# The forgetting heads' bias: a running sum on VectorE instead of a bias matmul per score block

## The chip, the core and the metric

The kernel runs on one core of one Trainium2 chip. A core has several engines that work side by side, each through its own list of instructions in order: TensorE (PE, matrix products, with its weight loads shown apart as PEld), VectorE (DVE), ScalarE (ACT), GpSimd (POOL), and SyncE (SP), which here does nothing but start transfers between DRAM and the on-chip memory SBUF. Matrix products end in PSUM, eight banks of 128 partitions by 512 numbers. The metric is the device time of one execution in microseconds; less is better.

## The reference

One layer of a hybrid sequence mixer, on 512 frames of width 2048, in float32. The normalised input is projected into three branches of four heads each (head width 128). Branch A is forgetting attention, the one that this change is in:

```python
log_f = jax.nn.log_sigmoid(f_logit)            # one logit per frame and head
c = jnp.cumsum(log_f, axis=1)                  # over the frames
logits = q @ k.T * scale                       # per block of 128 queries, keys 0..hi
logits = logits + c[lo:hi, None] - c[None, :hi]
logits = jnp.where(mask, logits, NEG)          # causal
o = softmax(logits) @ v
```

So the score of query t and key s carries c[t] − c[s], where c is the running sum of the log forget gates. Branch B is chunked attention with a learned bias by relative distance; branch C is stick-breaking attention. Each branch output is multiplied by the SiLU of a gate path and projected up to 2048 channels (the up stage), the three are merged with sigmoid gates, and one output projection with a residual ends the layer.

## The kernel before, in words

Activations lie with channels on the 128 partitions and the 512 frames along the free axis, so a tile is 128 by 512. Float32 accuracy is reached by splitting a number into a rounded part and a rest: ScalarE writes the rounded part (`hi`, line 243), VectorE the rest (`lo`, line 247), and a product is hi·hi + hi·lo + lo·hi. Nearly all of the vector and scalar work is these splits, of the weights above all: `wh` and `wl` for each weight tile `raw` that SP (or POOL, for tiles that are added together on their way) brings from DRAM. The large products run in pairs of column blocks with a Strassen-like scheme; line 262 holds their matmuls.

The program's order on PE, ACT and DVE is written out by a planner, `Flow`. Each piece of work is a Python generator that yields what it needs next: an event, slots of a pool, or an engine and a cost estimate. At every step the planner takes the piece that can start first on its engine. Pools of slots limit what is alive: 21 tiles of 256 KB (`t2s`), four PSUM banks for attention (`atts`), and others for weights and for the parts of the activations. Weight tiles form one long list of units; heads, gates and other work are hung at points of that list.

The stages in time: the start (to about 65 us), four C heads, four B heads (about 420 to 760 us), four A heads (about 760 to 1045 us), the up stage (to about 1205 us), and the output projections. Within the heads the score work is a small part between large projections, which fill TensorE. In the up stage each of 16 channel blocks is multiplied by its gate (line 1417) and summed over the branches (line 1424); two blocks are merged into a pair (`merged_a`, `merged_b`: the tiles `m`, `mt`, `mu`), which the output projections read.

The bias of an A head was made like this. `forget_bias` (in the first C head) writes the log forget gates of all heads to DRAM, `fd2`. `forget_sums`, shortly before the first A head, reads them, sums along the frames with a scan on VectorE (line 854), splits the sums, and lays them out in two tiles that stay to the end of the program: `crl` and `crb`. Rows 0 to 63 and 64 to 127 of these hold the parts of c and rows of ones, so that a product of the two, limited to one head's rows, gives c[t] − c[s]. `soft_start`, once per A head, makes that limit: `cr` is `crb` scaled on ScalarE by the head's column of a one-hot table `ohf` (line 968). `soft_scores`, once per block of 128 queries with m = 128, 256, 384 or 512 keys, issues the three matmuls of the scores, the bias matmul of `crl` and `cr` (line 992), the mask matmul (line 993, bfloat16), the row maximum on VectorE straight from PSUM (line 996), and the exponential on ScalarE from PSUM into `p` (line 998). A later division scales `p` (line 1014), and TensorE transposes it (line 1025).

A B head has no bias matmul: it fetches a tile `tb` of biases (256 KB) on SP, and one fused operation on VectorE adds `tb` to the scores, writes the sum to `p` in SBUF and gives the row maximum (line 1003, two instructions in the trace); line 1005 negates the maximum, and the exponential reads `p` (line 1008).

Of the kernel before, what the change touches and what calls it, by code (L numbers as in the profile page):

```python
# [12 lines left out]
ALU = mybir.AluOpType  # L13
# [49 lines left out]
class Flow:  # L63
# [16 lines left out]
    def give(self, slots, n=1):  # L80
        slots.free += [self.fin] * n
# [80 lines left out]
def hybrid_kernel(  # L162
# [34 lines left out]
    def t2(s, dt=F32):  # L197
        return tp.tile([P, S], dt, tag="t2", name=nm(s))
# [38 lines left out]
    def pair_of(name, dt=F32R):  # L237
        return t2(name + "h", dt), t2(name + "l", dt)
# [92 lines left out]

    ohf = cp.tile([P, NH], F32, name="ohf")
    nc.gpsimd.memset(ohf, 0.0)
    for r in range(4):
        nc.gpsimd.affine_select(out=ohf[32 * r:32 * r + 32, :], in_=ohf[32 * r:32 * r + 32, :],
                                pattern=[[1, NH]], base=0, channel_multiplier=-1,
                                compare_op=ALU.not_equal, fill=1.0)
# [470 lines left out]
    bias, bias_ev, f_ev, f2_ev = {}, Event(), Event(), Event()  # L808
    fd, fd2 = dp.tile([2 * NH, S], F32, name="fd"), dp.tile([NH, S], F32, name="fd2")

    def forget_bias():
# [25 lines left out]
        yield DVE, 3 * q  # L837
        nc.vector.scalar_tensor_tensor(p, p, 1.0, s, op0=ALU.add, op1=ALU.mult)
        nc.vector.tensor_scalar_mul(p, p, 2.0)
        nc.vector.scalar_tensor_tensor(v, v, 0.0, p, op0=ALU.min, op1=ALU.subtract)  # L840
        nc.sync.dma_start(fd2.rearrange("h (c t) -> (h c) t", t=T), v)
        f2_ev.t = flow.fin + 3.0

    def forget_sums():
        yield f2_ev
        yield t2s, 3
        v, s, u = t2("fv"), t2("fs"), t2("fu")
        nc.gpsimd.memset(v, 0.0)
        nc.gpsimd.memset(u, 1.0)
        for r in range(4):  # L850
# [3 lines left out]
        nc.vector.tensor_tensor_scan(s, u, v, 0.0, op0=ALU.mult, op1=ALU.add)  # L854
        give(t2s)
        yield t2s, 2
        hi, lo = pair_of("c")
        yield from split(hi, lo, s, S)
        give(t2s)
        yield t2s, 2  # L860
        crl, crb = t2("crl", F32R), t2("crb")
        a = ACT, act_us(S)
        yield a
        nc.scalar.activation(crl[0:32, :], f(hi[0:32, :]), AF.Copy)
        yield a
        nc.scalar.activation(crl[32:64, :], f(lo[32:64, :]), AF.Copy)
        yield a
        nc.scalar.activation(crl[64:128, :], u[64:128, :], AF.Copy)
        nc.gpsimd.memset(crb[0:64, :], 1.0)
        yield a  # L870
        nc.scalar.activation(crb[64:96, :], f(hi[64:96, :]), AF.Copy, scale=-1.0)
        yield a
        nc.scalar.activation(crb[96:128, :], f(lo[96:128, :]), AF.Copy, scale=-1.0)
        give(t2s, 3)
        bias["crl"], bias["crb"] = crl, crb
        set_(bias_ev)
# [8 lines left out]
    class Head:  # L885
# [74 lines left out]
        def soft_start(self):  # L960
            n = self.n
            yield from self.turn()
            yield t2s, 4
            if n == A:
                yield bias_ev
                self.bias = t2("cr", F32R)
                yield ACT, act_us(S)
                nc.scalar.activation(self.bias, bias["crb"], AF.Copy, scale=ohf[:, self.h:self.h + 1])
                set_(self.event("b"))
            else:  # L970
                self.bias = t2("tb")
                ev = fetch(self.bias, rel[self.h], flow.now, 256)
                yield ev
                yield DVE, 0.15
                nc.vector.memset(self.bias[0:64, S - 64:], NEG)
                set_(self.event("b"))
            self.p = tri("p")[::-1]

        def soft_scores(self, i):
# [6 lines left out]
            yield PE, mm_us(m, 3) + (mm_us(m) + mm_us(P) if n == A else 0)  # L986
# [4 lines left out]
            if n == A:  # L991
                nc.tensor.matmul(ps, bias["crl"][:, blk(i)], self.bias[:, :m], start=False, stop=False)
                nc.tensor.matmul(ps[:, blk(i)], identb, mska, start=False, stop=True)
                done = self.nth("s", QB)
                yield DVE, dve_us(m)
                nc.vector.tensor_reduce(mx, ps, axis=AX.X, op=ALU.max, negate=True)
                yield ACT, act_us(m) + 0.25
                nc.scalar.activation(p, ps, AF.Exp, bias=mx, accum_out=sm)
                give(atts)
            else:  # L1000
                done = self.nth("s", QB)
                yield DVE, dve_us(m) + 0.15
                nc.vector.tensor_tensor_reduce(out=p, in0=ps, in1=self.bias[:, S - m:], scale=1.0,
                                               scalar=-3e38, op0=ALU.add, op1=ALU.max, accum_out=mx)
                nc.vector.tensor_scalar_mul(mx, mx, -1.0)
                give(atts)
                yield ACT, act_us(m) + 0.25
                nc.scalar.activation(p, p, AF.Exp, bias=mx, accum_out=sm)
# [317 lines left out]
    for n, h in [(C, 1), (C, 2), (C, 3)] + [(n, h) for n in (B, A) for h in range(NH)]:  # L1326
        if (n, h) == (A, 0):
            at(len(units) - 4, forget_sums)
        last_head = head(n, h, (n, h) == (A, NH - 1))
# [306 lines left out]
```

## Time and profile before

| | |
|---|---|
| median of three runs | 1358.31 us |
| the three runs | 1358.43, 1358.31, 1356.82 us |
| span of the profiled execution (its only time on the page) | 1356.7 us |
| TensorE busy | 1334.7 us, 98% |
| VectorE busy | 1105.1 us, 81% |
| ScalarE busy | 802.8 us, 59% |
| GpSimd busy | 94.2 us, 7% |
| mean granted TensorE clock | 0.997 |

A row of a group or source view reads: line of the kernel, engine, operation, what is written and what is read, times it occurs, and the shortest, median and longest duration in ns. A row of the timeline reads: start in us, duration in us, then engine, line and operation; "x5" at its end says that five such instructions are put together, and a bracket says how long the engine was idle before it and what ended that. Durations of neighbouring instructions overlap, since an engine takes the next while the last one drains; the distance between two starts is what an instruction costs in a full engine.

### The profile page before, as it was taken

To read this page: it belongs to the slowest core of one execution; us is meant where nothing else is said; L and a number is where in the kernel's file an instruction comes from. 1 tells how busy PE (TensorE), PEld (TensorE's weight loads), DVE (VectorE), ACT (ScalarE), POOL (GpSimd) and SP (SyncE) were. 2 spreads that over 40 slices of the span, in tenths; PEclk is the share of its full clock that TensorE was granted. 3 is DMA by queue.
4 is the path that set the end of the run, shared out by engine and by line. 5 is a ranking of instruction groups with operands and counts; after the bars stand their busy time and mean duration, and the time that the engine had idled before them with its cause. 6 is when DMAs were issued, how large, how long until landed. Compare 5 with 4: busy or idle time off the path is not lost.

```text
span 1356.7 us, 19786 instructions
## 1 busy us (share of the span) xinstructions
PE 1334.7 (98%) x7394; PEld 1157.1 (85%) x7394; DVE 1105.1 (81%) x1592; ACT 802.8 (59%) x1240; POOL 94.2 (7%) x125
## 2 busy tenths in 40 slices
PE   7999999999999999999999999999999999989998
PEld 5788888888888888888888888888888788878887
DVE  5898997978878788787888878778787877888786
ACT  6655765646565566655667556665566655454443
POOL 0000000000100001000010000100000000000100
PEclk9999999999999999999999999999999999989999
DMA  9555667677677777777767777677767755748893
GB/s 328 170 145 151 178 163 197 169 209 192 173 189 204 196 205 172 193 198 200 201 171 196 186 193 201 168 186 199 184 182 248 252 187 181 209 127 246 237 243 95
DMA packets 91056, 262.01 MB, mean 193 GB/s; under 512 B 10168, under 2 KB 16440, under 8 KB 90960
## 3 DMA queue, kind: packets, MB, share of 16 engines
q1 hardware_dynamic: 72384, 201.96, 44.5%
q0 software_dynamic: 14976, 54.53, 24.3%
q10 hardware_dynamic: 3600, 4.26, 0.9%
q8 instruction: 58, 0.95, 0.3%
q14 instruction: 38, 0.31, 0.1%
HBM read 241.03 MB, written 19.69 MB: 192 GB/s over the span
## 4 chain that ended last, share of the span: by engine, by line
PE 96%; DVE 2%; DMA 0%; issue 0%; ACT 0%; SPq 0%; DVEq 0%; ACTq 0%
PE acc L262 82%; PE att L262 8%; DVE wl L247 1%; PE att L1096 1%; PE att L1025 1%; DVE m L247 1%; PE att L1164 1%; PE att L1163 1%; PE att L258 1%; PE att L259 1%; PE att L257 1%; PE att L1162 1%; DMA x<-in_xT 0%; PE att L1123 0%; PE att L923 0%
## 5 line engine op out<-in xcount | busy, mean ns | idle before, releaser
L247 DVE TENSOR_TENSOR wl<-raw,wh 128x1024 fp32r<-128x1024 f32 (+1 forms) x412 | 493.6, 1199 | 156.6 <-ACT wh L243 153.7
L243 ACT ACTIVATE wh<-raw 128x1024 fp32r<-128x1024 f32 (+1 forms) x412 | 427.2, 1038 | 148.6 <-PE acc L262 68.6
L262 PE MATMUL acc<-x,wh 128*128 128x512 f32 x1600 | 417.5, 396 | 9.9 <-ACT wh L243 9.9
L262 PEld LDWEIGHTS acc<-x,wh 128*128 128x128 f32 x1600 | 286.5, 189 | 61.6 <-ACT wh L243 9.9
L262 PE MATMUL acc<-t,wh 128*128 128x512 f32 x1056 | 273.7, 395 | 0.0
L262 PEld LDWEIGHTS acc<-x,wl 128*128 128x128 f32 x1504 | 210.5, 190 | 18.9
L262 PE MATMUL acc<-x,wl 128*128 128x256 f32 (+1 forms) x1504 | 223.6, 289 | 0.0
L262 PEld LDWEIGHTS acc<-t,wh 128*128 128x128 f32 x1056 | 187.5, 189 | 31.3
L262 PEld LDWEIGHTS acc<-t,wl 128*128 128x128 f32 x1056 | 145.1, 190 | 11.1
L262 PE MATMUL acc<-t,wl 128*128 128x256 f32 x1056 | 148.6, 282 | 0.0
L278 POOL DMA_DIRECT2D raw<-in_w_col x88 | 76.0, 864 | 941.0 <-DMA raw<-in_w_col 482.4
L262 PE MATMUL acc<-m,wh 128*128 128x512 f32 x448 | 114.4, 398 | 6.4 <-DVE m L247 6.0
L262 PEld LDWEIGHTS acc<-m,wh 128*128 128x128 f32 x448 | 81.8, 192 | 21.8 <-DVE m L247 6.4
L757 ACT ACTIVATE c<-acc 128x256 f32<-128x256 f32 x50 | 19.2, 383 | 104.2 <-PE acc L262 99.2
L735 ACT ACTIVATE u<-acc 128x512 f32<-128x512 f32 x50 | 29.8, 597 | 73.3 <-PE acc L262 73.3
L262 PE MATMUL att<-y,wh 128*128 128x512 f32 x256 | 66.6, 391 | 1.3 <-DVE y L247 1.3
L262 PEld LDWEIGHTS acc<-m,wl 128*128 128x128 f32 x448 | 62.1, 193 | 5.2 <-DVE wl L247 0.8
L262 PE MATMUL acc<-m,wl 128*128 128x256 f32 x448 | 63.4, 285 | 0.4 <-DVE wl L247 0.4
L641 DVE TENSOR_TENSOR raw<-raw,raw 128x1024 f32<-128x1024 f32 x52 | 63.4, 1219 | 0.4
L647 DVE TENSOR_TENSOR raw<-raw,raw 128x1024 f32<-128x1024 f32 x52 | 63.3, 1218 | 0.3
L718 ACT ACTIVATE v<-acc 128x512 f32<-128x512 f32 x52 | 31.1, 598 | 49.4 <-PE acc L262 46.1
L262 PEld LDWEIGHTS att<-y,wh 128*128 128x128 f32 x256 | 47.9, 188 | 12.2 <-DVE y L247 2.4
(211 smaller groups left out, 1408.9 us busy)
## 6 DMA issues: line engine op xcount, KB each, us to landing
raw<-in_w_col SPq DMA_DIRECT2D x236, 512.0 KB, 4.3
raw<-in_w_col POOLq DMA_DIRECT2D x88, 512.0 KB, 6.1
raw<-in_w_out SPq DMA_DIRECT2D x40, 512.0 KB, 4.5
gl<-c SPq DMA_DIRECT2D x48, 256.0 KB, 2.6
raw<-in_w_up SPq DMA_DIRECT2D x32, 384.0 KB, 3.2
sg<-gl SPq DMA_DIRECT2D x48, 256.0 KB, 4.7
raw<-in_w_out POOLq DMA_DIRECT2D x16, 512.0 KB, 6.2
x<-in_xT SPq DMA_DIRECT2D x16, 256.0 KB, 7.0
```

The source lines that it names most:

```text
L243: nc.scalar.activation(hi, src, AF.Copy)
L247: nc.vector.tensor_sub(lo, src, f(hi))
L257: nc.tensor.matmul(ps, lh, rh, start=start, stop=False, skip_group_check=more)
L258: nc.tensor.matmul(ps, lh, rl, start=False, stop=False, skip_group_check=more)
L259: nc.tensor.matmul(ps, ll, rh, start=False, stop=stop, skip_group_check=more)
L262: nc.tensor.matmul(ps, w, x, start=start, stop=stop, skip_group_check=more)
L278: nc.gpsimd.dma_start(to, src, accum_op=ALU.add)
L641: nc.vector.tensor_add(w[1], w[1], w[5])
L647: nc.vector.tensor_add(w[2], w[2], w[1])
L718: nc.scalar.activation(self.v, ps, AF.Copy)
L735: nc.scalar.activation(self.u, ps, AF.Copy)
L757: nc.scalar.activation(c, ps[:, RH], AF.Copy, scale=-1.0)
```

## The change

`forget_sums` is removed, with `crl`, `crb`, `ohf` and the bias matmul. `forget_bias` now stores −log f. Each A head fetches its own row of `fd2`, read into all 128 partitions, on SP's queue, and a scan on VectorE sums it in place: each element is the sum so far plus the element, and the maximum of that with the element itself, which for values that are not negative is the running sum. That is −c[s] in every partition. The fused add-and-maximum of B heads adds it to the scores. The term c[t], the same for a whole row of scores, is left out, since a softmax doesn't change by it. The mask matmul stays.

```diff
-    ohf = cp.tile([P, NH], F32, name="ohf")
-    nc.gpsimd.memset(ohf, 0.0)
...
     def forget_bias():
...
-        yield DVE, 3 * q
+        yield DVE, 4 * q
         nc.vector.scalar_tensor_tensor(p, p, 1.0, s, op0=ALU.add, op1=ALU.mult)
         nc.vector.tensor_scalar_mul(p, p, 2.0)
-        nc.vector.scalar_tensor_tensor(v, v, 0.0, p, op0=ALU.min, op1=ALU.subtract)
+        nc.vector.tensor_scalar(v, v, -1.0, 0.0, op0=ALU.mult, op1=ALU.max)
+        nc.vector.tensor_add(v, v, p)
         nc.sync.dma_start(fd2.rearrange("h (c t) -> (h c) t", t=T), v)
         f2_ev.t = flow.fin + 3.0
-
-    def forget_sums():
-        yield f2_ev
-        yield t2s, 3
-        v, s, u = t2("fv"), t2("fs"), t2("fu")
...
-        for r in range(4):
-            nc.sync.dma_start(v[32 * r:32 * r + NH, :], fd2)
-        yield Event(flow.now + 6.0)
-        yield DVE, 1.2
-        nc.vector.tensor_tensor_scan(s, u, v, 0.0, op0=ALU.mult, op1=ALU.add)
...
-        crl, crb = t2("crl", F32R), t2("crb")
...
-        bias["crl"], bias["crb"] = crl, crb
-        set_(bias_ev)
...
             if n == A:
-                yield bias_ev
-                self.bias = t2("cr", F32R)
-                yield ACT, act_us(S)
-                nc.scalar.activation(self.bias, bias["crb"], AF.Copy, scale=ohf[:, self.h:self.h + 1])
+                yield f2_ev
+                b = self.bias = t2("cr")
+                ev = fetch(b, fd2[self.h:self.h + 1, :].to_broadcast([P, S]), flow.now, 256)
+                yield ev
+                yield DVE, dve_us(2 * S)
+                nc.vector.tensor_tensor_scan(b, b, b, 0.0, op0=ALU.add, op1=ALU.max)
                 set_(self.event("b"))
...
-            yield PE, mm_us(m, 3) + (mm_us(m) + mm_us(P) if n == A else 0)
+            yield PE, mm_us(m, 3) + (mm_us(P) if n == A else 0)
...
             if n == A:
-                nc.tensor.matmul(ps, bias["crl"][:, blk(i)], self.bias[:, :m], start=False, stop=False)
                 nc.tensor.matmul(ps[:, blk(i)], identb, mska, start=False, stop=True)
-                done = self.nth("s", QB)
-                yield DVE, dve_us(m)
-                nc.vector.tensor_reduce(mx, ps, axis=AX.X, op=ALU.max, negate=True)
-                yield ACT, act_us(m) + 0.25
-                nc.scalar.activation(p, ps, AF.Exp, bias=mx, accum_out=sm)
-                give(atts)
-            else:
...
+            done = self.nth("s", QB)
+            yield DVE, dve_us(m) + 0.15
+            b = self.bias[:, :m] if n == A else self.bias[:, S - m:]
+            nc.vector.tensor_tensor_reduce(out=p, in0=ps, in1=b, scale=1.0, scalar=-3e38, op0=ALU.add, op1=ALU.max,
+                                           accum_out=mx)
+            nc.vector.tensor_scalar_mul(mx, mx, -1.0)
+            give(atts)
+            yield ACT, act_us(m) + 0.25
+            nc.scalar.activation(p, p, AF.Exp, bias=mx, accum_out=sm)
```

The planner's order moves with it. Three places follow, each before and then after. Rows give the line, the operation, what is written from what, and the size; the numbers at the names tell tiles apart and differ between the two kernels. Lines behind the removed functions have lower numbers after (1417 becomes 1370, 1003 becomes 958).

First TensorE at the second score block of the first A head (`acc` is the projection that runs beside it, `att` the scores, `qkh` and `qkl` the parts of q and k, `identb` and `mska` the mask's factors). Before:

```order
L262 MATMUL acc_7654<-x_12_144,wh_7652 128x512
L257 MATMUL att_7722<-qkh_7471,qkh_7636 128x256
L258 MATMUL att_7722<-qkl_7472,qkh_7636 128x256
L259 MATMUL att_7722<-qkh_7471,qkl_7637 128x256
L992 MATMUL att_7722<-cr_7617,crl_7196 128x256
L993 LDWEIGHTS identb
L993 MATMUL att_7722<-mska,identb 128x128
L262 MATMUL acc_7654<-x_13_145,wh_7652 128x512
```

After:

```order
L262 MATMUL acc_7616<-x_12_130,wh_7614 128x512
L257 MATMUL att_7685<-qkh_7436,qkh_7598 128x256
L258 MATMUL att_7685<-qkl_7437,qkh_7598 128x256
L259 MATMUL att_7685<-qkh_7436,qkl_7599 128x256
L954 LDWEIGHTS identb
L954 MATMUL att_7685<-mska,identb 128x128
L262 MATMUL acc_7616<-x_13_131,wh_7614 128x512
```

The bias matmul is gone, and the projection around the block stands where it stood.

Second VectorE at the first score block of the same head (`mx` is the maximum, `cr` the bias; the operation on `cr` at line 930 is the scan). Before:

```order
L247 TENSOR_TENSOR qkl_7637<-rs_7446,qkh_7636 128x512
L247 TENSOR_TENSOR wl_7653<-raw_7408,wh_7652 128x1024
L996 TENSOR_REDUCE mx_7688<-att_7684 128x1
L247 TENSOR_TENSOR wl_7679<-raw_7482,wh_7678 128x1024
```

After:

```order
L247 TENSOR_TENSOR qkl_7599<-rs_7411,qkh_7598 128x512
L247 TENSOR_TENSOR wl_7615<-raw_7373,wh_7614 128x1024
L930 SCALAR_TENSOR_TENSOR cr_7582<-cr_7582 128x512
L247 TENSOR_TENSOR wl_7641<-raw_7447,wh_7640 128x1024
L958 ISA p_7651,mx_7670<-att_7666,cr_7582 128x128
L958 ISA mx_7670 128x1
L960 TENSOR_SCALAR mx_7670<-mx_7670 128x1
```

The scan stands between two weight splits, and the second of these now comes ahead of the maximum.

Third VectorE between the up stage and the output projections, from the last product with a gate to the last merged tile (`sg` are the gated blocks, `mt` and `mu` the merged pair of the last two blocks, `m` its parts). The subtractions at line 253 into `mt` and `mu` are what differs. Before, the last rows of the stretch:

```order
L247 TENSOR_TENSOR m_2166_11874<-mu_11389,m_2166_11874 128x256
L253 SCALAR_TENSOR_TENSOR mt_11805<-mt_11805,sg_11553 128x256
L247 TENSOR_TENSOR m_2166_11874<-mu_11389,m_2166_11874 128x256
L247 TENSOR_TENSOR m_2173_11910<-mu_11715,m_2173_11910 128x256
L253 SCALAR_TENSOR_TENSOR mu_11715<-mt_11805,sg_11622 128x256
L247 TENSOR_TENSOR m_2180_11954<-mt_11805,m_2180_11954 128x2x256
```

After:

```order
L247 TENSOR_TENSOR m_2164_11862<-mu_11358,m_2164_11862 128x256
L253 SCALAR_TENSOR_TENSOR mu_11641<-mt_11773,sg_11591 128x256
L247 TENSOR_TENSOR m_2164_11862<-mu_11358,m_2164_11862 128x256
L247 TENSOR_TENSOR m_2166_11880<-mu_11641,m_2166_11880 128x256
L247 TENSOR_TENSOR m_2173_11921<-mt_11773,m_2173_11921 128x2x256
```

One subtraction into `mt` has moved ahead, out of these rows, and the other two operations of the pair have changed places with splits beside them; all of them still stand between the last gated product and the last `m`. The pair before it, of the seventh block, moves farther. Before:

```order
L253 SCALAR_TENSOR_TENSOR mt_11671<-mt_11671,sg_11411 128x256
L641 TENSOR_TENSOR raw_11573<-raw_11573,raw_11536 128x1024
L1417 TENSOR_TENSOR sg_11622<-acc_11725,sg_11622 128x512
L1443 TENSOR_TENSOR sg_11553<-sg_11553 128x256
L253 SCALAR_TENSOR_TENSOR mu_11715<-mt_11671,sg_11483 128x256
```

After:

```order
L247 TENSOR_TENSOR m_2119_11642<-sg_11452,m_2119_11642 128x2x256
L1370 TENSOR_TENSOR sg_11522<-acc_11630,sg_11522 128x512
L253 SCALAR_TENSOR_TENSOR mt_11640<-sg_11452,sg_11380 128x256
L253 SCALAR_TENSOR_TENSOR mt_11640<-mt_11640,sg_11380 128x256
L253 SCALAR_TENSOR_TENSOR mu_11641<-mt_11640,sg_11452 128x256
L247 TENSOR_TENSOR wl_11667<-raw_11469,wh_11666 128x768
```

Before, the second `mt` and `mu` of the seventh block stood among the work on the last pair (the product of `acc` with `sg_11622` is the last block's first); now they stand directly behind the first, one block earlier.

More of the change, by code (lines that the diff above doesn't have):

```diff
@@ L330, in hybrid_kernel @@
     nc.vector.tensor_copy(mskc, zerof)
-    ohf = cp.tile([P, NH], F32, name="ohf")
-    nc.gpsimd.memset(ohf, 0.0)
-    for r in range(4):
-        nc.gpsimd.affine_select(out=ohf[32 * r:32 * r + 32, :], in_=ohf[32 * r:32 * r + 32, :],
-                                pattern=[[1, NH]], base=0, channel_multiplier=-1,
-                                compare_op=ALU.not_equal, fill=1.0)
     gq = cp.tile([P, 4], F32, name="gq")
@@ L807, in hybrid_kernel @@
     yd = {}
-    bias, bias_ev, f_ev, f2_ev = {}, Event(), Event(), Event()
+    f_ev, f2_ev = Event(), Event()
     fd, fd2 = dp.tile([2 * NH, S], F32, name="fd"), dp.tile([NH, S], F32, name="fd2")
@@ L1326, in hybrid_kernel @@
     for n, h in [(C, 1), (C, 2), (C, 3)] + [(n, h) for n in (B, A) for h in range(NH)]:
-        if (n, h) == (A, 0):
-            at(len(units) - 4, forget_sums)
         last_head = head(n, h, (n, h) == (A, NH - 1))
```

30 lines of the change are left out of this document (removed).

## The prediction

> **What bounds the kernel now.** I read the page's shares and its chain of waits first, then the matrix engine's own waits, then stretches of equal work.
>
> ```profile
> span 1356.7 us, 19786 instructions
> PE 1334.7 (98%) x7394; PEld 1157.1 (85%) x7394; DVE 1105.1 (81%) x1592; ACT 802.8 (59%) x1240; POOL 94.2 (7%) x125
> PE 96%; DVE 2%; DMA 0%; issue 0%; ACT 0%; SPq 0%; DVEq 0%; ACTq 0%
> ```
>
> TensorE is 96% of the chain that ended last. A chain that blames a full engine says little about a stretch with gaps, so the next view lists where TensorE had nothing to run:
>
> ```profile
> PE acc L262 <- ACT wh L243: 10.3, 2, 9.9
> PE acc L262 <- DVE m L247: 6.0, 1, 6.0
> PE att L262 <- DVE y L247: 1.3, 2, 1.0
> ```
>
> The columns are us in total, times, and the longest. The 10.3 us belong to the start, the 1.3 us to the start of the up projections, and one wait of 6.0 us stands between the up projections and the output projections. None of them is in a head. The windows view (us, then busy us of PE, PEld, DVE, ACT and POOL, granted clock, DMA share, GB/s) shows one B head, the stretch that holds `forget_sums`, and one A head:
>
> ```profile
> 505.00:590.00 85.00, 85.00 (x496) 74.91 (x495) 69.75 (x100) 52.91 (x80) 6.90 (x8) 1.00 0.73 193
> 674.00:759.50 85.50, 85.50 (x499) 75.35 (x498) 72.05 (x103) 57.12 (x88) 8.47 (x11) 1.00 0.73 195
> 845.00:930.00 85.00, 85.00 (x496) 74.51 (x495) 68.33 (x91) 52.62 (x80) 6.90 (x8) 1.00 0.72 185
> ```
>
> TensorE is busy for the whole of all three at full clock. So in an A head every matmul taken away shortens the program by its own spacing, and work taken from or given to the other engines counts only when it makes TensorE wait. The period of a head confirms the size of what is at stake, in the chain of waits (start, length, what), two pieces from B heads and two from A heads:
>
> ```profile
> 545.35 20.64 PE acc L262 x117
> 629.90 20.64 PE acc L262 x117
> ...
> 800.10 20.64 PE acc L262 x117
> ...
> 885.74 20.64 PE acc L262 x117
> ```
>
> A B head takes 629.90 − 545.35 = 84.55 us, an A head 885.74 − 800.10 = 85.64 us. The 1.09 us between them are what an A head's scores need beyond a B head's: the bias matmul and the mask matmul.
>
> **The sixteen bias matmuls.** This is the TensorE timeline of the second A head (start, length, instruction), the bias matmul and the mask matmul of each of its four score blocks:
>
> ```profile
> 848.44 0.27 PE L992 MATMUL att<-cr,crl 128*128 128x128 f32 x1
> 848.55 0.23 PE L993 MATMUL att<-mska,identb 128*128 128x128 bf16 x1
> ...
> 851.83 0.28 PE L992 MATMUL att<-cr,crl 128*128 128x256 f32 x1
> 851.95 0.23 PE L993 MATMUL att<-mska,identb 128*128 128x128 bf16 x1
> ...
> 855.41 0.34 PE L992 MATMUL att<-cr,crl 128*128 128x384 f32 x1
> 855.58 0.23 PE L993 MATMUL att<-mska,identb 128*128 128x128 bf16 x1
> ...
> 859.19 0.39 PE L992 MATMUL att<-cr,crl 128*128 128x512 f32 x1
> 859.42 0.23 PE L993 MATMUL att<-mska,identb 128*128 128x128 bf16 x1
> ```
>
> The lengths overlap, so what a matmul costs is the distance to the next start: 0.11, 0.12, 0.17 and 0.23, together 0.63 us per head. The other 0.46 us of the 1.09 belong to the mask, which stays. Four heads give 4 × 0.63 = **2.5 us**. The lower bound is nothing, should something other than TensorE set these stretches; the upper one 4 × 1.09 = 4.4 us, if the pause around each mask went as well. I take the spacing, since the engine has no gap there.
>
> [...]
>
> **What VectorE gets.** The diff's score block is the one that B heads already run, so B's rows price it (lowest, median, highest ns):
>
> ```profile
> L996 DVE TENSOR_REDUCE mx<-att x16: 284/487/692, 763.2 to 1022.6; 128x1 f32<-128x128 f32 x4, 128x1 f32<-128x256 f32 x4, 128x1 f32<-128x384 f32 x4, 128x1 f32<-128x512 f32 x4
> L1003 DVE CUSTOM_DVE_ANT_0 p<-att,tb x16: 283/477/684, 426.5 to 690.1; 128x128 f32<-128x128 f32 x4, 128x256 f32<-128x256 f32 x4, 128x384 f32<-128x384 f32 x4, 128x512 f32<-128x512 f32 x4
> L1003 DVE DVE_READ_ACCUMULATOR2_ANT mx<- x16: 81/82/84, 426.8 to 690.7; 128x1 f32 x16
> L1005 DVE TENSOR_SCALAR mx<-mx x16: 153/153/154, 426.9 to 690.8; 128x1 f32<-128x1 f32 x16
> L854 DVE TENSOR_TENSOR_SCAN fs<-fu,fv x1: 1217/1217/1217, 704.8 to 704.8; 128x512 f32<-128x512 f32 x1
> ```
>
> The add-and-maximum costs what the plain maximum did (477 against 487 ns). New are the read of the accumulator and the negation, 4 × (0.082 + 0.153) = 0.94 us per head, and one running sum over 128x512, 1.22 us: 2.2 us per head. VectorE goes from 68.3 to 70.5 us in 85. A B head carries 69.75 and the `forget_sums` stretch 72.05 with no gap on TensorE, so that cover hides it and I cost it at nothing. Without the cover it would be 4 × 2.2 = 8.6 us.
>
> **What ScalarE gets and loses.** The scaled copy that made `cr` goes, and the exponential reads SBUF in place of PSUM, as in B heads, where ScalarE is at 52.91 of 85 with no gap on TensorE (52.62 in an A head now): nothing on the path. The PSUM bank comes free one exponential earlier; no wait for a bank is in the list above, so nothing again.
>
> **What leaves before the A heads.** `forget_sums` (the scan, a split, five copies, memsets, four DMAs) falls in the middle window, where TensorE is full at 85.50 of 85.50: nothing. The one extra operation on 128x16 in `forget_bias` stands in a C head, where the list of waits has none for TensorE; the one-hot table `ohf` is built at the start, where TensorE waits 10.3 us for `wh`, not for it. Nothing for both.
>
> **The row in all partitions.** Each A head now fetches one 2 KB row of DRAM into 128 partitions, 256 KB on SP's queue, then sums in place.
>
> ```profile
> tb<-in_rel SPq DMA_DIRECT2D x4, 256.0 KB, 3.5
> x<-in_xT SPq DMA_DIRECT2D x16, 256.0 KB, 7.0
> ...
> 749.21 3.53 SPq L1203 DMA_DIRECT2D gl<-c x2
> ...
> 760.78 1.23 DVE L247 TENSOR_TENSOR wl<-raw,wh 128x1024 fp32r<-128x1024 f32 x1 [0.82 <-ACT wh L243]
> 763.16 0.29 DVE L996 TENSOR_REDUCE mx<-att 128x1 f32<-128x128 f32 x1 [1.16 <-PE att L993]
> 763.58 1.22 DVE L247 TENSOR_TENSOR wl<-raw,wh 128x1024 fp32r<-128x1024 f32 x1
> ...
> 771.20 1.11 PE L262 MATMUL acc<-t,wl 128*128 128x256 f32 x8
> ```
>
> In the new order the fetch stands right behind these two `gl` stores, about 752.7; the scan stands behind the split at 760.78, so about 761.95, and fits the idle 1.16 us ahead of the first maximum. That leaves 9.2 us for a landing that takes 3.5 us for a bias tile of the same size from DRAM and 7.0 us at the slowest 256 KB group. No row shows a broadcast source; between 3.5 and 7.0 I take 3.5, and either is covered. On SP, three weight loads stand behind the fetch; they also stood behind B's fetch, in heads without a gap.
>
> **The end of the last A head.** Its four score blocks now follow each other closely, and the transposes on TensorE wait for all four.
>
> ```profile
> 1026.07 0.72 ACT L1014 ACTIVATE p<-p,sm 128x512 f32<-128x512 f32 x1 [0.67 <-DVE sm L1012]
> ...
> 1028.04 0.60 PE L1025 MATMUL att<-identf,p 128*128 128x128 f32 x4
> ```
>
> Now the last scaled block is there at 1026.79, 1.25 us ahead of the transposes. Four blocks each with 0.235 us more on VectorE shorten that to 0.3 us if they run strictly in series. I cost it at nothing; the other bound is about 1 us late.
>
> **The step to the output projections.** Two 256 KB tiles (`crl`, `crb`) are no longer kept to the end, so the merging of the last channel blocks can start earlier in the written order. The 6.0 us wait is for the last of these merged tiles, `m`:
>
> ```profile
> 1184.92 1.07 PE L262 MATMUL att<-y,wl 128*128 128x512 f32 x4
> ...
> 1204.71 0.79 PE L262 MATMUL acc<-m,wh 128*128 128x512 f32 x1 [5.96 <-DVE m L247]
> ...
> 1180.34 0.42 DVE L253 SCALAR_TENSOR_TENSOR mt<-mt,sg 128x256 f32<-128x256 f32 x1
> ...
> 1186.14 0.68 DVE L1417 TENSOR_TENSOR sg<-att,sg 128x512 f32<-128x512 f32 x1
> ...
> 1206.00:1216.00 10.00, 10.00 (x46) 8.60 (x46) 7.83 (x12) 2.72 (x3) 0.86 (x1) 0.77 0.83 195
> ```
>
> In the new order two subtractions of the seventh block, into `mt` (1180.34) and `mu`, 0.33 us to the next start each, have moved up past several operations, so VectorE comes to the last gated product (1186.14) 0.67 us earlier. But that product needs TensorE's last up matmul, which ends at 1185.99, so VectorE can gain 1186.14 − 1185.99 less a hand-over of some 0.04, 0.1 us; from there to `m` the same operations follow. Bounds: 0 and 0.67 us. I take **0.1 us**.
>
> **The sum.** −2.53 − 0.11 = −2.6 us: the span goes from 1356.7 to 1354.1. The page gives no other time of the profiled execution. The three runs (1358.43, 1358.31, 1356.82) lie 0.1 to 1.7 us above its span, 1.15 in the mean, so I lay the difference on their mean, 1357.85: **1355.2 us**; laid on the median it would be 1355.7.
>
> **Rivals.**
>
> *The wait before the output projections shrinks more.* If the 0.67 us come through in full, the gain is 3.2 us. The granted clock after that wait is 0.77 for 10 us, 2.3 us lost; if a shorter wait also spared that, 5.5 us in all: **1352.4**. For it speaks that VectorE works without a gap up to `m`; against it the product that TensorE still holds back, and a wait that would still be over 5 us.
>
> [...]
>
> *The gain is eaten on the way.* Either the last head's transposes come up to 1 us late, or the waits at the start of the up projections (1.3 us), which VectorE ends, grow by what TensorE arrives earlier: VectorE has 1 us more in that head. **1356.2 to 1357.9**. For it: the 0.3 us of slack in the strict series; against it: VectorE is idle for a microsecond several times in every head, and arrives earlier too, since its inputs come from TensorE.
>
> *Slower: the scan holds VectorE.* The scan is an in-order wait for a DMA; behind it on VectorE stands the split at 763.58, done at 764.8, which TensorE needs at 771.20 (the `wl` half of the fold behind the third score block). So VectorE can stand for 6.4 us beyond the 9.2, and from a landing of about 15.5 us on every further microsecond costs TensorE one, in each of four heads. If 128 reads of one DRAM row took five times the 3.5 us, 17.5 us, it is 4 × 2 − 2.6 = +5.4 us: **1363.2**. For it: no row has such a source. Against it: it needs over twice the slowest 256 KB group.
>
> *The change does nothing of the kind it says* is out: in the written order the sixteen matmuls are gone.
>
> **How the numbers follow.** Chances: my forecast 0.55 (its own range 1354.2 to 1356.2, from the place of the runs above the span and a bias term up to a sixth smaller), the larger shrinking 0.12, the eaten gain 0.27, the late row 0.06. The range 1352.6 to 1357.6 leaves out the late row, the top of the eaten gain (0.06) and the low half of the first rival (0.06). About 0.2%, 2.7 us, is what can be told from no change. From 1358.31 that is 1355.6: two thirds of the forecast and the first rival lie below, 0.37 + 0.12, so faster 0.49; the rest of the forecast and nearly all of the eaten gain is 0.44; slower 0.07.
>
> **What would show it.** The period of an A head should read 85.0 us in the chain of waits, 0.63 shorter, and TensorE full in an A head's window with VectorE near 70.5 of 85. The fetch should land in 3 to 7 us, and the scan have no wait for it. The transposes of the last head should show no wait, and the wait for `m` read 5.8 to 6.0 us. Wrong would be an A head with a gap on TensorE, a scan that waits for DMA, or a wait for `m` that has moved by over half a microsecond.

## The result, and the profile after

The changed kernel takes 1354.55 us (median of 8 runs, 1353.45 to 1355.01) where the kernel before takes 1357.78 us (median of 8 runs): a ratio of 0.9978, 95% interval 0.9969 to 0.9986. By the medians it is faster by 3.2 us; the interval allows 1.9 to 4.2. The prediction had 1355.2 us.

The page's span, engines and chain:

```profile
span 1352.2 us, 19771 instructions
PE 1330.0 (98%) x7378; PEld 1154.2 (85%) x7378; DVE 1110.0 (82%) x1627; ACT 798.0 (59%) x1230; POOL 92.0 (7%) x117
```

TensorE has 16 instructions fewer and is 4.7 us less busy, VectorE has 4.9 us more and ScalarE 4.8 us less. TensorE's own waits are the same four as before:

```profile
PE acc L262 <- ACT wh L243: 10.6, 2, 10.2
PE acc L262 <- DVE m L247: 5.9, 1, 5.9
PE att L262 <- DVE y L247: 1.3, 2, 1.0
PE acc L262 <- DVE wl L247: 0.4, 1, 0.4
```

The chain of waits, two pieces from neighbouring B heads and two from neighbouring A heads, then the windows view of the second A head:

```profile
544.42 20.64 PE acc L262 x117
628.99 20.64 PE acc L262 x117
...
798.59 20.64 PE acc L262 x117
883.62 20.64 PE acc L262 x117
...
845.00:930.00 85.00, 85.00 (x495) 74.56 (x494) 70.50 (x100) 52.76 (x79) 6.90 (x8) 1.00 0.74 193
```

A B head still takes 84.57 us. An A head takes 883.62 − 798.59 = 85.03 us in place of 85.64, and TensorE is still full in it, with VectorE at 70.50 of 85 us.

**Two profiles differ by more than the program.** The spans differ by 1356.7 − 1352.2 = 4.5 us, more than the medians. Three pieces can be told apart in the chain: up to the long piece of the first B head; from there to the end of the wait for `m` ahead of the output projections; and the rest. For the two kernels, and for four profiles of the first group of experiments below:

| profile of | span | first B head's piece at | to the end of the wait for `m` | behind that wait |
|---|---|---|---|---|
| before | 1356.7 | 460.82 | 743.89 | 151.99 |
| the change | 1352.2 | 459.86 | 741.33 | 151.01 |
| the change, again | 1351.8 | 459.51 | 741.34 | 150.95 |
| before, no bias matmul | 1352.6 | 460.06 | 741.40 | 151.14 |
| the change, matmul put back | 1355.8 | 460.19 | 743.86 | 151.75 |
| the change, two tiles kept | 1352.5 | 459.90 | 741.49 | 151.11 |

The middle part repeats to 0.01 us in two profiles of one kernel, and it falls by 743.89 − 741.33 = **2.56 us**. That is less than the 3.2 us of the medians; beside thirty more runs of the kernel before (median 1357.18 us), eleven of the changed kernel had a median of 1354.64 us, 2.5 us less. So 2.56 us can be placed in the program, and nothing here traces the rest of the 3.2.

The first and the last part differ over 1.3 and 1.0 us in this table. One kernel's executions differ that much: the spans of those thirty runs lie from 1354.6 to 1356.8 us. In the table the two kernels with the bias matmul, or one like it, have the longest last parts, but the matmul doesn't set them: the kernel with the mask in the bias too (below) has none and needs 152.08 us behind a wait of 5.86.

In the last part it is the clock that differs. The first eight microseconds behind the wait, in four-microsecond windows (columns as above), of the kernel before, of the changed kernel, and of the one with the matmul put back:

```profile
1204.71:1208.71 4.00, 4.00 (x13) 3.52 (x14) 1.68 (x4) 1.06 (x1) 0.00 (x0) 0.50 0.89 229
1208.71:1212.71 4.00, 4.00 (x19) 3.39 (x18) 3.18 (x5) 1.06 (x1) 0.86 (x1) 0.77 0.68 206
```

```profile
1201.19:1205.19 4.00, 4.00 (x14) 3.57 (x15) 1.67 (x4) 1.06 (x1) 0.00 (x0) 0.54 0.87 223
1205.19:1209.19 4.00, 4.00 (x25) 3.50 (x24) 3.93 (x7) 1.06 (x1) 0.41 (x1) 1.00 0.76 222
```

```profile
1204.05:1208.05 4.00, 4.00 (x13) 3.52 (x14) 1.67 (x4) 1.06 (x1) 0.00 (x0) 0.50 0.93 206
1208.05:1212.05 4.00, 4.00 (x20) 3.40 (x19) 3.38 (x5) 1.06 (x1) 0.86 (x1) 0.82 0.70 226
```

The clock granted is half, or nearly, in the first window of each, and comes back after 4 to 6 us, at another moment in each of these three profiles. The kernel with the matmul put back waits 5.86 us, as the changed kernel does, and still keeps the low clock nearly as long as the kernel before.

The first part varies in a like manner. From 12 to 16 us TensorE issues 11 matmuls before and 15 in the changed kernel, 16 in its second profile, and 13 and 14 in the other kernels without the one-hot table's work; 14 also in the kernel that still has that work (before, no bias matmul). All of them wait about 10 us for the first weights. The clock column of the windows view shows 1.00 there, so that the array is slow is read from the count and the spacing alone: two 128x512 matmuls of the kernel before take 0.85 us at first and 0.46 later, from start to start. That this is the clock too is inferred.

### The profile page after: what moved, and what is told of

Read it like the earlier page. It is cut to its first block, busy times and chain, and to the rows that moved or that the text cites. A ratio compares the mean times of both kernels' runs of the same rounds, so it can differ in the third digit from the quotient of the medians.

```text
span 1352.2 us, 19771 instructions
## 1 busy us (share of the span) xinstructions
PE 1330.0 (98%) x7378; PEld 1154.2 (85%) x7378; DVE 1110.0 (82%) x1627; ACT 798.0 (59%) x1230; POOL 92.0 (7%) x117
## 4 chain that ended last, share of the span: by engine, by line
PE 98%; DVE 1%; DMA 0%; ACT 0%; issue 0%; SPq 0%; DVEq 0%; ACTq 0%
PE acc L262 84%; PE att L262 9%; PE att L1051 1%; PE att L980 1%; PE att L1119 1%; PE att L1118 1%; PE att L258 1%; PE att L259 1%; PE att L257 1%; PE att L1117 1%; DMA x<-in_xT 0%; DVE wl L247 0%; PE att L1078 0%; PE att L884 0%; PE att L883 0%; DVE m L247 0%
```

## The experiments

Each was timed beside the kernel before on the same chip, and the ratios are to that. There were three such groups; the kernel before had medians of 1357.18 us (30 runs) in the first, 1357.23 (16) in the second, which holds the extra scans, the mask in the bias and the eight half tiles, and 1357.09 (9) in the third.

### Is the gain the sixteen matmuls?

The changed kernel once more.

> The changed kernel itself, once more. The two profiled spans lie 4.5 us apart (1356.7 and 1352.2), the sum of the prediction was 2.6. Theory T1: the program's own gain is about 2.5 us, and the other 1.9 us are the granted clock at two places, the first 6 us of TensorE (low until about 16.0 us before, 13.9 us in the changed kernel) and the stretch behind the 6 us wait ahead of the output projections; these vary from execution to execution of one kernel, so this profile shows the low stretch at the start with another length, a span anywhere in 1351.5 to 1353.5, A heads of 85.0 us and a wait for m of 5.9 us. Theory T2: the start and the stretch behind the wait are shorter because the change removed work there, so this profile shows both as short as the first one did, within 0.2 us.

Measured: 1354.64 us, ratio 0.9979 (0.9971 to 0.9988). The span of this profile is 1351.8; the A heads take 85.03 us, the wait for `m` 5.86 us, and TensorE issues 16 matmuls from 12 to 16 us. The middle part is 741.34 us. The start is 0.35 us shorter than in the first profile, more than T2 allowed; behind the wait the two profiles differ by 0.06 us only, so for that stretch this run alone doesn't decide between T1 and T2.

The kernel before without the bias matmul:

```diff
-                nc.tensor.matmul(ps, bias["crl"][:, blk(i)], self.bias[:, :m], start=False, stop=False)
```

> The kernel before without the sixteen bias matmuls, all else left as it is (the forget bias is left out of the scores, the sums and tiles for it are still made). T1: the A heads take 85.0 us in place of 85.64, the time is 2.5 us under before, the same as the changed kernel within 0.3 us. T2: 2.5 us here too, but 0.7 to 2 us above the changed kernel, because the start and the end keep what they had. A third case, TensorE not the bound in the A heads: less than 1.5 us gained here.

Measured: 1354.29 us, ratio 0.9976 (0.9967 to 0.9986), 0.35 us under the changed kernel and not to be told from it. Two A heads in its chain of waits:

```profile
798.71 20.64 PE acc L262 x117
883.73 20.64 PE acc L262 x117
```

85.02 us. The middle part falls by 743.89 − 741.40 = 2.49 us; the forecast for the matmuls was 2.53. So this one line carries the gain. All of the old work is still in it, and yet its start (460.06 us) and its stretch behind the wait (151.14 us) are near those of the changed kernel and not of the kernel before: T2 is out. The `forget_sums` work, the one-hot table, the two kept tiles and the scaled copies, all still in this kernel, cost it nothing that can be seen.

The changed kernel with a matmul of the same form added to each score block:

```diff
+                nc.tensor.matmul(ps, ql[:, blk(i)], kl[:, :m], start=False, stop=False)
                 nc.tensor.matmul(ps[:, blk(i)], identb, mska, start=False, stop=True)
```

> The changed kernel with one more matmul per score block of an A head, of the same type and size as the removed one (the product of the two lo parts of q and k, added to the scores). T1: the A heads take 85.6 to 85.7 us again, and the time is 2.5 us over the changed kernel, within 0.4 us of before. T2: about 1 to 2 us stay gained against before.

Measured: 1356.53 us, ratio 0.9996 (0.9987 to 1.0005). The middle part is back at 743.86 us, 0.03 us from the kernel before, and an A head takes 85.67 us:

```profile
799.56 20.64 PE acc L262 x117
885.23 20.64 PE acc L262 x117
```

By the medians only 1.9 us came back of 2.5, and the time is 0.65 us under the kernel before, where T1 had allowed 0.4; medians of ten runs with a spread of 2 us don't settle half a microsecond, the middle parts do.

The changed kernel with two tile slots held from the first A head on, so that the order ahead of the output projections is the old one:

```diff
+    def two_kept():
+        yield t2s, 2
...
+        if (n, h) == (A, 0):
+            at(len(units) - 4, two_kept)
```

> The changed kernel with two of the 21 tile slots taken from the first A head to the end, so that the order of VectorE's work between the up stage and the output projections is that of before. T1: the wait for m is 5.96 us in place of 5.87, the time 0.1 us over the changed kernel, which no run can tell. T2: the wait or the low clock behind it grows by 0.5 us or more, and the time with it.

Measured: 1354.21 us, ratio 0.9977 (0.9967 to 0.9986). TensorE's row at the wait, with this kernel and then with the changed one:

```profile
1201.39 0.80 PE L262 MATMUL acc<-m,wh 128*128 128x512 f32 x1 [5.97 <-DVE m L247]
```

```profile
1201.19 0.80 PE L262 MATMUL acc<-m,wh 128*128 128x512 f32 x1 [5.87 <-DVE m L247]
```

The two freed tiles are worth the 0.1 us that was forecast, and the middle part agrees (741.49 against 741.33 us).

### How long may VectorE stand at the scan?

The slower rival held that VectorE can stand 6.4 us there before TensorE notices. Extra scans ahead of the one that counts, written to a tile that is overwritten later, stand in for a row that lands late:

```diff
+                self.p = tri("p")[::-1]
+                for _ in range(4):
+                    nc.vector.tensor_tensor_scan(self.p[3], b, b, 0.0, op0=ALU.add, op1=ALU.max)
                 nc.vector.tensor_tensor_scan(b, b, b, 0.0, op0=ALU.add, op1=ALU.max)
```

> The changed kernel with four more scans of the same row in each A head ahead of the one that counts, written to a tile that is overwritten later: VectorE stands 4 x 1.22 = 4.9 us longer at that place in each of four heads, and is busy 75.4 of 85 us in a head. By the prediction's slower rival VectorE can stand 6.4 us there before TensorE misses its next split weights: no loss, the time of the changed kernel within 0.5 us. Rival: another result of VectorE is needed sooner (a PSUM bank that it has to read out, or the maxima of the scores), and TensorE stands 1 to 4 us per head, 4 to 16 us in all.

Measured: 1371.47 us, ratio 1.0106 (1.0092 to 1.012), about 17 us above the changed kernel: the rival of an earlier deadline, and a little more than the 16 us that it had at most. Two of TensorE's waits in this kernel are new:

```profile
PE acc L262 <- DVE v L732: 6.0, 3, 2.0
...
PE att L259 <- DVE qkl L247: 3.8, 1, 3.8
```

Here are the scans on VectorE in the first A head, what stands behind them, and what TensorE waits for:

```profile
761.56 4.99 DVE L932 TENSOR_TENSOR_SCAN p<-cr 128x512 f32<-128x512 f32 x4
766.59 1.22 DVE L933 TENSOR_TENSOR_SCAN cr<-cr 128x512 f32<-128x512 f32 x1
...
769.24 0.68 DVE L732 TENSOR_TENSOR v<-v,acc 128x512 f32<-128x512 f32 x1
...
770.07 0.93 PE L262 MATMUL acc<-t,wh 128*128 128x512 f32 x3 [1.99 <-DVE v L732]
```

The operation at line 732 reads a projection out of PSUM, and the next projection needs that bank. Only four instructions stand between the scan and it. 4.9 us more on VectorE became 2.0 us of waiting on TensorE, so **2.9 us** is what VectorE may stand there, not 6.4. The waits sum to 9.8 us and the loss is 17: part of the rest is the clock behind these waits. The windows of the first and of the second A head around the 1.99 us wait:

```profile
767.00:771.00 4.00, 2.01 (x13) 1.71 (x12) 3.90 (x11) 0.55 (x3) 0.00 (x0) 1.00 0.78 166
771.00:775.00 4.00, 4.00 (x24) 3.18 (x23) 3.97 (x6) 1.90 (x4) 0.86 (x1) 1.00 0.25 82
856.00:860.00 4.00, 2.66 (x9) 2.12 (x10) 3.90 (x12) 1.65 (x6) 0.00 (x0) 0.74 0.45 135
860.00:864.00 4.00, 4.00 (x21) 3.23 (x20) 3.97 (x7) 1.84 (x4) 0.86 (x1) 0.83 0.42 54
```

The same wait of 1.99 us left the clock at full rate in the first head and lowered it in the second; in the third it was 0.71 and 0.86 in the windows from 945 to 953 us. The second and the third A head take 88.83 us each, 3.80 more than in the changed kernel, and 1.99 of that is the wait.

With eight extra scans:

> The same with eight more scans, 9.8 us per head, VectorE busy 80.3 of 85 us. By the prediction's 6.4 us TensorE stands about 3.0 to 3.4 us in each of four heads, 12 to 14 us in all, and the waits of TensorE name the split weights (wl). Rival with an earlier deadline: 5 to 9 us per head, 20 to 36 us in all. If the stand was fully covered by idle time in the head (15 us), nothing.

Measured: 1394.84 us, ratio 1.0278 (1.0264 to 1.0292). The same two waits:

```profile
PE acc L262 <- DVE v L732: 21.1, 3, 7.0
...
PE att L259 <- DVE qkl L247: 8.8, 1, 8.8
```

7.0 us per head out of 9.8, again 2.8 less than what was added. No new wait names `wl`, so the 6.4 us are out here too. The waits sum to 29.9 us, as the rival had it; the loss is 40 us, above its 20 to 36. In the last A head the scan stands elsewhere in the order, ahead of a split of k and q that the scores need (`qkl`), with about 1 us to spare (4.9 − 3.8 and 9.8 − 8.8).

### The mask goes into the bias too

What an A head still has beyond a B head is the mask matmul. The bias row lies in SBUF now, so VectorE can add the mask to it, if the score blocks run from the longest to the shortest: each block masks its own 128 columns, which no later block reads. The last A head is left as it was.

```diff
+            fold = n == A and not self.last
+            if fold:
+                if i < QB - 1:
+                    yield self.event("m", i + 1)
+                b = self.bias[:, blk(i)]
+                yield DVE, dve_us(P)
+                nc.vector.tensor_add(b, b, mska)
...
-            if n == A:
+            if n == A and not fold:
                 nc.tensor.matmul(ps[:, blk(i)], identb, mska, start=False, stop=True)
...
+            set_(self.event("m", i))
...
-                g += [(s + i, one(self.soft_scores, i)) for i in range(QB)]
+                g += [(s + i, one(self.soft_scores, QB - 1 - i if self.n == A and not self.last else i)) for i in range(QB)]
```

> The changed kernel with the mask matmul gone too in the first three A heads: the score blocks run from the longest to the shortest, and before each VectorE adds the causal mask to that block's 128 columns of the bias row, four small additions per head. If the remaining difference between an A and a B head (85.03 against 84.57 us) is the mask matmul, the three heads take 84.57 us and the time is 1.4 us under the changed kernel. Rival: the larger blocks first, or the additions, make TensorE wait, and the gain is under 0.5 us or a loss.

Measured: 1352.66 us, ratio 0.9966 (0.9954 to 0.9978). Two A heads and the window of one:

```profile
804.32 14.59 PE acc L262 x83
888.78 14.59 PE acc L262 x83
...
845.00:930.00 85.00, 85.00 (x497) 75.10 (x496) 71.84 (x104) 52.28 (x79) 6.91 (x8) 1.00 0.71 192
```

A head takes 84.46 us, 0.57 less than with the mask matmul, where the difference to a B head had promised 0.46. VectorE carries 71.84 us with no gap on TensorE. The middle part is 1199.72 − 460.13 = 739.59 us, 1.74 under the changed kernel.

### The wait ahead of the output projections

Here the order was changed on top of the last kernel, to see whether the place of the last `m` on VectorE sets the wait, or all that VectorE has to do there. First the last `mt` (its two subtractions and its split) ahead of the rest, and nothing taken away:

```diff
-        yield q
+        last = k == UK - 1
+        q1 = (*q, 0.0) if last else q
+        yield q1
         minus(t[:, LH], b[:, RH], a[:, RH])
-        yield q
+        yield q1
         minus(t[:, RH], t[:, LH], a[:, LH])
...
-        yield from split(m23[k].hi, m23[k].lo, two(t), S, ev, (due + 7.0,))
+        yield from split(m23[k].hi, m23[k].lo, two(t), S, ev, (0.0 if last else due + 7.0,))
+        if last:
+            yield (*q, due + 8.0)
+            minus(u, t[:, LH], b[:, LH])
```

> The kernel with the mask in the bias, and only the order of VectorE's work ahead of the output projections changed: the two subtractions and the split of the last mt come before the work that they stood behind, nothing is taken from VectorE. If the place of that one operation sets the 5.9 us wait, the wait goes and the time falls by 5 us or more against the kernel with the mask alone (1352.66). If VectorE's whole backlog sets it, the wait for m goes but other waits (split weights, the half tiles from mu) take its place, 5 to 7 us in all, and the time stays within 1 us, with at most 2 us gained where no single wait is long enough to lower the clock.

Measured: 1351.56 us, ratio 0.9960 (0.9946 to 0.9973). The wait for `m` is gone, and three others stand in its place:

```profile
1192.41 1.22 PE L262 MATMUL acc<-m,wl 128*128 128x256 f32 x8 [1.54 <-DVE wl L247]
1210.03 2.11 PE L262 MATMUL acc<-m,wh 128*128 128x512 f32 x8 [2.44 <-ACT wh L243]
1214.31 1.43 PE L262 MATMUL acc<-m,wl 128*128 128x256 f32 x8 [2.17 <-DVE wl L247]
```

They sum to 6.15 us where one wait of 5.86 us stood. So the place of that one operation doesn't set the loss: with it out of the way, other work comes late by as much. Two of the three waits are for VectorE. The one for `wh` is for ScalarE, which had just waited twice for VectorE itself (0.73 and 0.74 us); how much of that one goes back to VectorE's backlog is not shown. The median is 1.1 us lower, in another group and with intervals that cover each other; what would explain it is the clock, which from 1198 to 1218 us is 0.93 with the shorter waits and 0.83 with the mask alone (first this kernel, then that one):

```profile
1198.00:1218.00 20.00, 15.39 (x80) 12.97 (x79) 16.70 (x24) 6.26 (x7) 1.72 (x2) 0.93 0.75 207
```

```profile
1198.00:1218.00 20.00, 18.28 (x90) 16.03 (x91) 16.21 (x26) 6.23 (x8) 1.31 (x2) 0.83 0.67 173
```

Then, on top of that order, work taken from VectorE as well: the rest parts of the half tiles from `mu` on GpSimd. The kernel with all eight of them there was run before the one above.

```diff
-        yield from split(h, lo, u, HS, ev, (due + 14.0,))
+        yield (ACT, act_us(HS), due + 14.0)
+        nc.scalar.activation(h, u, AF.Copy)
+        nc.gpsimd.tensor_sub(lo, u, f(h))
...
```

> As the one with the mask in the bias, and two changes for the wait ahead of the output projections: the rest parts of the eight half tiles from mu are computed on GpSimd, not on VectorE (8 x 0.33 us less there), and the two subtractions and the split of the last mt come first in VectorE's order. If VectorE's work in that stretch sets the wait, the 5.9 us shrink by 2.7 us and fall into two or three shorter waits, and the time is 3 to 4 us under the one with the mask alone, more (up to 6) where the clock stays high. Rival: the place of the last m in the order sets it, and the wait goes away by itself: more than 5 us. Third: GpSimd is slow, and TensorE waits for it instead: no gain or a loss.

Measured, for all eight: 1355.02 us, ratio 0.9987 (0.9978 to 0.9996), 2.4 us worse than the mask alone.

```profile
PE acc L262 <- POOL m L1454: 2.7, 4, 1.2
...
1190.84 13.56 POOL L1454 TENSOR_TENSOR m<-mu,m 128x256 fp32r<-128x256 f32 x8 [12.49 <-ACT m L1453]
```

GpSimd needs 13.56 us for eight, and TensorE waits for it: the third case. With four of the eight:

> The same with the rest parts of four of the eight half tiles on GpSimd, which took 1.70 us for each where VectorE takes 0.34: VectorE is relieved of 1.4 us, GpSimd is done after 6.8 us. If VectorE's backlog sets the waits and GpSimd is early enough, 1 us better than with the order alone. If VectorE is slowed while GpSimd works (a 128x256 operation took 0.84 us then, not 0.41), no gain.

Measured: 1351.04 us, ratio 0.9958 (0.9946 to 0.9971). TensorE doesn't wait for GpSimd, which does four in 4.30 us; with the order alone it was 1351.56, and the two intervals cover each other. VectorE got no relief: its next six splits of `m`, most of which run beside GpSimd's four, take longer (first with the order alone, then with the four on GpSimd):

```profile
1185.72 3.69 DVE L247 TENSOR_TENSOR m<-mt,m 128x512 fp32r<-128x512 f32 x6
```

```profile
1186.11 5.34 DVE L247 TENSOR_TENSOR m<-mt,m 128x512 fp32r<-128x512 f32 x6
```

They lose 1.65 us where 1.4 us were taken away, as the expectation's last case had it. TensorE's waits in the stretch sum to 5.29 us all the same, 0.86 less than with the order alone; the runs don't show why. Whether the four on GpSimd bring anything is open. Both kernels lie below the changed one, at 1351.6 and 1351.0 against 1354.6 us, and their intervals (up to 0.9973 and 0.9971) end about where its own begins (0.9971).

## Why the prediction was right

**The sixteen bias matmuls, forecast 2.53 us: right.** An A head lost 0.61 us (forecast 0.63), the line alone 2.49 us, and putting a like matmul back cost 743.86 − 741.34 = 2.52 us. The distance from one start to the next was the right price here, where TensorE is full.

**What VectorE got, costed at nothing: right.** Its time in the head's window is 70.50 us (forecast 70.5). The scan costs what the one scan of the kernel before cost, and the add-and-maximum what it costs in B heads:

```profile
L930 DVE TENSOR_TENSOR_SCAN cr<-cr x4: 1217/1219/1219, 761.0 to 1013.5; 128x512 f32<-128x512 f32 x4
L958 DVE CUSTOM_DVE_ANT_0 p<-att,cr x16: 292/488/684, 764.0 to 1019.7; 128x128 f32<-128x128 f32 x4, 128x256 f32<-128x256 f32 x4, 128x384 f32<-128x384 f32 x4, 128x512 f32<-128x512 f32 x4
```

**What left ahead of the A heads, costed at nothing: right.** The kernel that keeps all of it and lacks only the matmuls is as fast.

**The row in all partitions: hidden, as forecast.** Its landing, its place on SP, and the scan in the changed kernel:

```profile
cr<-fd SPq DMA_DIRECT2D x4, 256.0 KB, 5.0
...
751.94 0.38 SPq L274 DMA_DIRECT2D cr<-fd  x1
...
761.04 1.22 DVE L930 TENSOR_TENSOR_SCAN cr<-cr 128x512 f32<-128x512 f32 x1
```

The median landing, 5.0 us, lies between the bounds of 3.5 and 7.0, where 3.5 had been taken, and the slowest of the four took 7.0; 9.1 us were there. VectorE's list of waits has none for the scan.

**The end of the last head, costed at nothing: right, with more to spare than the strict series had.**

```profile
1022.32 1.61 ACT L969 ACTIVATE p<-p,sm 128x256 f32<-128x256 f32 x3
...
1024.90 0.60 PE L980 MATMUL att<-identf,p 128*128 128x128 f32 x4
```

The last scaled block is there at 1023.93, 0.97 us ahead of the transposes; the bound had 0.3. The four blocks overlap on ScalarE and VectorE.

**The step to the output projections, forecast 0.1 us: right**, 5.87 against 5.96 us, and 5.97 with the old order put back. The reason given holds too: VectorE now stands and waits for TensorE's last up matmul ahead of the last gated product.

```profile
1181.50 1.07 PE L262 MATMUL att<-y,wl 128*128 128x512 f32 x4
...
1182.61 0.69 DVE L1370 TENSOR_TENSOR sg<-att,sg 128x512 f32<-128x512 f32 x1 [0.47 <-PE att L262]
```

The matmuls end at 1182.57, and the product starts 0.04 us later, the hand-over that had been taken.

**The sum, −2.6 us.** The middle part shows 2.56. That the forecast of 1355.2 us came within 0.65 us of the median owes something to the draw: the medians of these runs lie 3.2 us apart, and the part of it above 2.56 is in no term.

**What was wrong.** Three numbers that the sum didn't rest on. First, the place of the runs above the span: every run's time is 1.7 to 1.9 us above its own span (1353.89 for 1352.2, 1357.53 for 1355.8), and the three runs lay 0.1 to 1.7 us above the span shown because the spans of the executions differ, in the profiles above at the start and behind the wait. By this the profiled execution before stood near 1358.4, at the top of the runs. Laying the difference on the mean of the runs was the right choice, for another reason than the one given. Second, the slower rival's 6.4 us: it took the next split weights for the first thing that TensorE misses, and overlooked the read-out of a PSUM bank (line 732) behind the scan. The measured figure is 2.9 us, so in the first three heads a row would begin to hurt at about 9.1 + 2.9 = 12 us after its fetch, an estimate from these rows, and not at 15.5. Third, the first rival's price. It tied the 2.3 us of lowered clock to the length of the wait; with waits of 5.86 to 5.97 us what lies behind the wait took 150.95 to 152.08 us, with no order by length. What a wait shorter by the rival's 0.67 us would spare, no run tested; with three shorter waits in its place the clock was higher, 0.93 against 0.83 over 20 us.

The rest of the mask, 0.46 us by subtraction of two periods, is not what came of taking it away: with the order of the blocks turned round as well, a head gained 0.57. Whether an A head has then less on TensorE than a B head, or the order around its blocks is better, the runs don't tell.

## What to carry to other kernels

Where TensorE is full, price a matmul by the distance to the next start (here 2.53 us for the sixteen, 2.49 measured), and look for the same addition on an engine with idle time: a bias that depends on the column alone needs no matmul, and what is constant along a softmax row needs nothing at all. For how long an engine may stand, follow every instruction behind the wait, the read-outs of PSUM first (here 2.9 us, not 6.4), and not only the stream that the other engine obviously lives on. Where runs differ by as much as the effect, compare the stretch of the chain between two fixed points of the program: here it repeated to 0.01 us when medians of ten runs left half a microsecond open.

## What the runs showed of the hardware

**Behind a wait of 2 us TensorE's granted clock was lower in two heads of three.** The 1.99 us wait at line 732 left the clock at 1.00 in one head, and it was 0.74 and 0.83 in two windows around and behind it in the next, 0.71 and 0.86 in the third. What decides whether the same wait acts, the runs don't show.

**Two sums on VectorE took 1.21 us beside GpSimd, 0.69 us without it.** In the kernel with all eight half tiles on GpSimd, VectorE's groups from 1197 to 1204.5 us (mean ns behind the comma), GpSimd being busy for the whole of 1196 to 1204 us:

```profile
L769 DVE TENSOR_TENSOR t<-t,u 128x512 f32<-128x512 f32 x1 | 1.2, 1208 | 0.0
L780 DVE TENSOR_TENSOR v<-v,u 128x512 f32<-128x512 f32 x1 | 1.2, 1207 | 0.0
...
L1483 DVE TENSOR_TENSOR c<-c,xr 128x512 f32<-128x512 f32 x1 | 0.7, 678 | 0.0
L764 DVE TENSOR_TENSOR u<-u,acc 128x512 f32<-128x512 f32 x1 | 0.7, 677 | 0.0
```

and in the second profile of the changed kernel:

```profile
L769 DVE TENSOR_TENSOR t<-t,u 128x512 f32<-128x512 f32 x1 | 0.7, 692 | 0.0
L780 DVE TENSOR_TENSOR v<-v,u 128x512 f32<-128x512 f32 x1 | 0.7, 691 | 0.0
L764 DVE TENSOR_TENSOR u<-u,acc 128x512 f32<-128x512 f32 x1 | 0.7, 687 | 2.3 <-PE acc L262 2.3
L1463 DVE TENSOR_TENSOR c<-c,xr 128x512 f32<-128x512 f32 x1 | 0.7, 684 | 0.0
```

The sums of two SBUF tiles at lines 769 and 780 took 1.21 us in place of 0.69; the one with an input from PSUM (line 764) was not slowed, 0.68 against 0.69. Nor was the sum at line 1483 (1463 in the changed kernel), whose inputs both lie in SBUF: 0.68 us in both, at 1202.02 us beside GpSimd. So two inputs in SBUF don't settle it, and what does, these rows don't show.
